# Seven products for eight: the in-projection of a state-space mixer in a part of its own

## The chip, the cores and the metric

The kernel runs on one core of a Trainium2 chip. The metric is the device time of one execution in microseconds; of a kernel the median of several executions is told. Before the change it was 983.28 us, the median of 3 runs (982.39 to 983.92). A core has five engines that run side by side, each with an in-order queue of its own: TensorE (PE, matmuls), VectorE (DVE), ScalarE (ACT), GpSimd (POOL) and SyncE (SP), which here issues all DMAs. Matmuls write to PSUM, eight banks of 512 fp32 columns on 128 partitions; all else lies in SBUF.

## The reference, cut to what matters

One layer of a bidirectional Mamba-2 mixer, all in float32, 1024 tokens, model width 1024, inner width 2048, 32 heads of 64 in 8 groups, state 128, chunks of 128 tokens:

```
u    = rmsnorm(x, norm_w)                            # (1024, 1024)
proj = u @ w_in                                      # z 2048 | x 2048 | B 1024 | C 1024 | dt 64
x, B, C = silu(conv5(x | B | C) + bias)              # depthwise, centred, over tokens
dt   = softplus(dt_raw + dt_bias);  a = -exp(a_log)
y    = x * D
for direction in (forward, backward):                # chunked scan, per group g and chunk c
    y += (C B^T * decay) @ (x dt)                    # inside a chunk, per head
    y += (C @ state) * exp(cumsum a)                 # from the chunks before
    state = state * chunk_decay + B^T @ (x dt decay)
y    = groupnorm(y * silu(z)) * norm
out  = rmsnorm(x + y @ w_out, final_norm_w)
```

## The kernel before, in words

A float32 product is made from three matmuls in the faster fp32r type: each operand is split into a high part (ACT casts it) and a low part (DVE subtracts), and hi*hi, hi*lo and lo*hi are added up in PSUM. The matmuls of the scan are plain fp32; each of them shows as two in the trace.

Start (`load_x` and the loop at L281): eight tiles of 128 tokens are normalised, transposed on PE (L295) and split into `us`, which holds u with channels on partitions for two halves of 512 tokens. Beside it the z product of group 0 runs, together with dt.

In-projection (`inproj`, a generator that is advanced piece by piece): for a group g the units B, C, x0, x1 (128 channels each: 2 halves x 8 k-tiles x 3 matmuls of 512 columns, L180) and z (`z_unit`, 8 token tiles x 24 matmuls of 256 columns, L157). `conv` takes a unit out of PSUM: ACT makes the middle tap (L190), DVE the four others straight from PSUM (L196, 1022 or 1023 columns), ACT a tanh (L199), DVE the closing product (L200). `load_split` (L122, L123) splits the weights, 1024 columns an operation.

Scan (`ssd_units(g)`): first backwards over the chunks, `token_major(c)` (three PE transposes of x0, x1, B, L404, and an ACT copy, L407), `state` (L390, L393) and `update` (L383, L385) for the backward direction; then forwards. `mix(c)` loads the rows of the decays as `fb`, broadcast over the partitions (two slots, L415), ACT adds (L419), DVE selects (L421), ACT takes the exponential (L424), and DVE multiplies with C B^T (L429). Then PE makes the state part `pyo` (L462) and the inner part `pyd` (L468), DVE and ACT put `y` together (L471, L479, L481), the gate (L486), ACT squares into `pyd` (L488), POOL takes the power -1/2 (L85), ACT scales (L490), DVE transposes blocks of 32 x 32 (L493) and SP writes y to DRAM in runs of 128 bytes (L496). PSUM: `ps_ip` has two slots of two banks, `ps_g` four of one bank for all else.

While group g is scanned, the projection of group g + 1 is pulled in after the steps named in `AT` (L501 to L507), so the two lie beside each other. In the last group's scan four token tiles of the out projection (`out_unit`, first half of k) are pulled in instead; the other 12 follow. The order of instructions on each engine is fixed when the program is made, by a planner that takes the program's order as priority; what stands under `tc.high_priority` goes ahead.

Of the kernel before, what the change touches and what calls it, by code (L numbers as in the profile page):

```python
# [31 lines left out]
def kernel(  # L32
# [25 lines left out]
    ps_g = ctx.enter_context(tc.tile_pool(name="ps_g", bufs=4, space=PSUM))  # L58
# [12 lines left out]
    cfb = const.tile([P, 2, NC, NH], F32, name="cfb")  # L71
    ecs = const.tile([P, 2, NC, NH], F32, name="ecs")
    wdt = const.tile([P, 2, NC, NH], F32, name="wdt")
    dcy = const.tile([P, 2, NC, NH], F32, name="dcy")
    dtb = const.tile([P, NC, NH], F32, name="dtb")

    rows_d = dram.tile([2 * NC * NH, P], F32, name="rows_d")
    y_d = dram.tile([DI, L], F32, name="y_d")

    def rstd_of(pool, ss, n, eps, name):  # L80
# [31 lines left out]

    def load_split(srcs, kk, n, name):
        raw = wp.tile([P, kk, n], F32, tag="raw", name=name + "r", bufs=2)
        at = 0
        for src in srcs:
            m = src.shape[2]
            nc.sync.dma_start(out=raw[:, :, at:at + m], in_=src)
            at += m
        hi = wp.tile([P, kk, n], R32, tag="wh", name=name + "h", bufs=4)  # L120
        lo = wp.tile([P, kk, n], R32, tag="wl", name=name + "l", bufs=4)
        nc.scalar.copy(hi, raw)  # L122
        nc.vector.tensor_tensor(out=lo, in0=raw, in1=hi.bitcast(F32), op=ALU.subtract)  # L123
        return hi, lo

    def load_cm(col, name):
        return load_split([w_in[:, :, col:col + P]], NK, P, name)

    def load_z(g):

        n, ks = (CW + 2 * NH, (0, 3, 6, 8)) if g == 0 else (CW, (0, 4, 8))
        at = []
        for i, (k0, k1) in enumerate(zip(ks, ks[1:])):
            srcs = [w_in[:, k0:k1, g * CW:(g + 1) * CW]]
            if g == 0:
# [7 lines left out]
    cms = {}  # L143

    def z_unit(g, c0, wz):

        w, n = (512, 2) if g == 0 else (CW, 4)
        pz = ps_ip.tile([P, n, w], F32, tag="ip", name=f"pz{g}_{c0}")
        m = CW + 2 * NH if g == 0 else CW
        for i in range(n):  # L150
            tok = slice((c0 + i) % 4 * P, ((c0 + i) % 4 + 1) * P)
            uh, ul = us[(c0 + i) // 4]
            at = 0
            for k in range(NK):
                hi, lo = wz[k]
                for a, b in ((uh, hi), (uh, lo), (ul, hi)):
                    nc.tensor.matmul(pz[:, i, 0:m], a[:, k, tok], b,  # L157
                                     start=at == 0, stop=at == 3 * NK - 1)
                    at += 1
        gt = gates[g, c0 // 4]  # L160
        pzg = pz[:, :, 0:CW]
        gt = gt[:, c0 % 4:c0 % 4 + n]
# [3 lines left out]
        if g == 0:  # L166
            for i in range(n):
                nc.vector.tensor_tensor(
                    out=v[:, :, c0 + i, :],
                    in0=pz[:, i, CW:CW + 2 * NH].rearrange("p (d h) -> p d h", d=2),  # L170
                    in1=dtbias, op=ALU.add)
        return n

    def cm_matmul(ps, w, half):
        hi, lo = w
        uh, ul = us[half]
        n = 0
        for k in range(NK):
            for a, b in ((hi, uh), (hi, ul), (lo, uh)):
# [470 lines left out]
```

## Time and profile before

| | |
|---|---|
| median of 3 runs | 983.28 us (982.39 to 983.92) |
| profiled execution | 985.42 us |
| its span, first to last instruction | 983.7 us |
| PE busy | 945.5 us, 96% |
| DVE busy | 727.9 us, 74% |
| ACT busy | 539.2 us, 55% |
| POOL busy | 53.8 us, 5% |
| granted clock of PE | 0.999 of full speed |
| moved by DMA | 107.62 MB, 16 engines busy 41.5% |

The busy time of an engine is the time in which at least one of its instructions ran; instructions of one engine overlap a little, matmuls a good deal, so that what one costs in a row of its like is read from the distance of their starts.

### The profile page before, as it was taken

Reading aid. Unit: us, or ns where it says so; the run is one execution under the profiler, and the core shown is the slowest. Engines: PE = TensorE matmul, PEld = TensorE weight load, DVE = VectorE, ACT = ScalarE, POOL = GpSimd, SP = SyncE. Lnnn points to the kernel's source line nnn. Section 1 sums busy time; section 2 is a strip of 40 time slices with the busy share of each in tenths; the row PEclk is TensorE's granted clock in tenths of the full one; section 3 lists DMA queues with packets and bytes.
Section 4 is the critical chain, followed back from the end, with each engine's and each line's share of the span. In section 5 each row is a group of like instructions: output and inputs, shape, how many; then the busy total and the mean of one; then the engine's idle time right before and its main releaser. Section 6 shows DMA issues by size and latency. Waiting matters only on the chain.

```text
span 983.7 us, 15133 instructions
## 1 busy us (share of the span) xinstructions
PE 945.5 (96%) x5220; PEld 806.1 (82%) x5220; DVE 727.9 (74%) x1552; ACT 539.2 (55%) x1458; POOL 53.8 (5%) x88
## 2 busy tenths in 40 slices
PE   5999999999999999999999999999999999999997
PEld 5987778877887798778887988788889878888886
DVE  4688889867986887688868886888688988552322
ACT  5435567636673767366736673676367876431211
POOL 1100000000000000000000100010001001000000
PEclk9999999999999999999999999999999999999999
DMA  7334134422452345134513352336325686684321
GB/s 223 95 86 97 43 70 94 111 70 70 101 120 53 74 99 124 49 75 98 126 52 82 86 129 63 78 80 126 96 64 142 172 264 174 200 278 142 118 85 65
DMA packets 157325, 107.62 MB, mean 109 GB/s; under 512 B 75248, under 2 KB 133312, under 8 KB 157248
## 3 DMA queue, kind: packets, MB, share of 16 engines
q1 hardware_dynamic: 157248, 106.65, 41.5%
q8 instruction: 41, 0.67, 0.3%
q14 instruction: 36, 0.29, 0.1%
HBM read 89.58 MB, written 17.04 MB: 108 GB/s over the span
## 4 chain that ended last, share of the span: by engine, by line
PE 56%; DVE 12%; DMA 12%; ACT 12%; issue 6%; POOL 2%; SPq 1%; DVEq 0%; POOLq 0%; ACTq 0%
PE po L562 16%; PE ipx L180 12%; PE ipC L180 9%; DMA fb<-rows_d 7%; PE ipB L180 7%; ACT yo L479 3%; DVE x L196 3%; ACT fb L424 2%; PE pz L157 2%; PE pyo L462 2%; PE pyd L468 2%; PE sb L393 2%; ACT fb L419 2%; DVE mt L429 1%; PE sf L393 1%
## 5 line engine op out<-in xcount | busy, mean ns | idle before, releaser
L479 ACT ACTIVATE yo<-pyo,ecs 128x64 f32<-128x64 f32 x448 | 103.1, 320 | 35.8 <-PE pyo L462 30.2
L419 ACT ACTIVATE fb<-fb,cfb 128x128 f32<-128x128 f32 x256 | 85.1, 399 | 55.1 <-DMA fb<-rows_d 49.6
L424 ACT ACTIVATE fb<-fb,cfb 128x128 f32<-128x128 f32 x256 | 84.0, 398 | 3.8 <-DVE fb L421 3.7
L196 DVE SCALAR_TENSOR_TENSOR x<-ipx,prm,x 128x1022 f32<-128x1022 f32 (+1 forms) x64 | 81.1, 1268 | 3.7 <-ACT x L190 3.6
L157 PE MATMUL pz<-wz_1l,uh 128*128 128x256 f32 (+1 forms) x248 | 73.0, 294 | 2.0 <-DVE wz_1l L123 2.0
L157 PE MATMUL pz<-wz_0h,ul 128*128 128x256 f32 (+1 forms) x248 | 73.3, 296 | 0.4 <-DVE ul L301 0.2
L157 PE MATMUL pz<-wz_0l,uh 128*128 128x256 f32 (+1 forms) x248 | 72.0, 290 | 0.0
L157 PE MATMUL pz<-wz_0h,uh 128*128 128x256 f32 (+1 forms) x248 | 71.2, 287 | 0.0
L157 PE MATMUL pz<-wz_1h,ul 128*128 128x256 f32 (+1 forms) x248 | 70.9, 286 | 0.0
L468 PEld LDWEIGHTS pyd<-xb,mt 128*128 128x128 f32 x512 | 66.7, 191 | 4.9 <-DVE mt L429 1.8
L157 PE MATMUL pz<-wz_1h,uh 128*128 128x256 f32 (+1 forms) x248 | 70.4, 284 | 0.0
L471 DVE SCALAR_TENSOR_TENSOR y<-xb,coef,pyd 128x64 f32<-128x64 f32 x256 | 62.5, 273 | 10.5 <-PE pyd L468 10.3
L468 PE MATMUL pyd<-xb,mt 128*128 128x64 f32 x512 | 64.7, 269 | 0.0
L429 DVE TENSOR_TENSOR mt<-fb,pcb 128x512 f32<-128x512 f32 x64 | 43.1, 681 | 15.3 <-PE pcb L427 13.0
L385 DVE TENSOR_TENSOR pb<-pb,sb 128x256 f32<-128x256 f32 x48 | 19.8, 412 | 42.0 <-PE sb L393 41.1
L421 DVE COPY_PREDICATED fb<-trif,fb 128x512 f32<-128x512 uint32 x64 | 47.1, 736 | 3.7 <-ACT fb L419 3.6
L157 PEld LDWEIGHTS pz<-wz_1l,uh 128*128 128x128 f32 x248 | 46.9, 189 | 3.4 <-DVE wz_1l L123 3.2
L157 PEld LDWEIGHTS pz<-wz_0h,ul 128*128 128x128 f32 x248 | 47.2, 190 | 1.3 <-DVE ul L301 1.1
L571 DVE TENSOR_TENSOR h<-po,h 128x1024 f32<-128x1024 f32 (+2 forms) x10 | 10.1, 1011 | 51.3 <-PE po L562 51.3
L157 PEld LDWEIGHTS pz<-wz_0h,uh 128*128 128x128 f32 x248 | 47.1, 190 | 0.5
L157 PEld LDWEIGHTS pz<-wz_0l,uh 128*128 128x128 f32 x248 | 47.1, 190 | 0.0
L157 PEld LDWEIGHTS pz<-wz_1h,ul 128*128 128x128 f32 x248 | 46.9, 189 | 0.2
(511 smaller groups left out, 2667.5 us busy)
## 6 DMA issues: line engine op xcount, KB each, us to landing
fb<-rows_d SPq DMA_DIRECT2D x128, 256.0 KB, 4.3
y_d<-yt SPq DMA_DIRECT2D x256, 32.0 KB, 2.0
wo<-in_ssd_w_out_dram SPq DMA_DIRECT2D x16, 512.0 KB, 4.2
yt<-y_d SPq DMA_DIRECT2D x16, 512.0 KB, 5.1
xt<-in_x_dram SPq DMA_DIRECT2D x8, 512.0 KB, 5.9
h<-in_x_dram SPq DMA_DIRECT2D x8, 512.0 KB, 4.8
h_d<-h SPq DMA_DIRECT2D x8, 512.0 KB, 3.0
h<-h_d SPq DMA_DIRECT2D x8, 512.0 KB, 3.6
```

The costliest lines, as they stand in the source:

```text
L157: nc.tensor.matmul(pz[:, i, 0:m], a[:, k, tok], b, start=at == 0, stop=at == 3 * NK - 1)
L180: nc.tensor.matmul(ps[:, half * 512:(half + 1) * 512], a[:, k, :], b[:, k, :], start=n == 0, stop=n == 3 * NK - 1)
L196: nc.vector.scalar_tensor_tensor(out=acc[:, o], in0=ps[:, i], scalar=w(k), in1=acc[:, o], op0=ALU.mult, op1=ALU.add)
L393: nc.tensor.matmul(ps[:, 0:CW], xb[:, CW:CW + P], xw, start=True, stop=True)
L419: nc.scalar.activation(out=ef[:, h], in_=ef[:, h], func=AF.Identity, bias=cfb[:, 1, c, hsl(g, h)])
L421: nc.vector.copy_predicated(ef, trif.bitcast(U32).unsqueeze(1).broadcast_to([P, HG, P]), fb[:, 0])
L424: nc.scalar.activation(out=ef[:, h], in_=ef[:, h], func=AF.Exp, bias=cfb[:, 0, c, hsl(g, h)])
L429: nc.vector.tensor_tensor(out=mt, in0=ef, in1=pcb[:, 0:P].unsqueeze(1).broadcast_to([P, HG, P]), op=ALU.mult)
L468: nc.tensor.matmul(pyd[:, cs], mt[:, h, :], xb[:, cs], start=True, stop=True)
L471: nc.vector.scalar_tensor_tensor(out=y[:, cs], in0=xb[:, cs], scalar=coef[:, h:h + 1], in1=pyd[:, cs], op0=ALU.mult, op1=ALU.add)
L479: nc.scalar.activation(out=yo[:, cs], in_=pyo[:, d * CW + h * HD:d * CW + (h + 1) * HD], func=AF.Copy, scale=ecs[:, d, c, hsl(g, h)])
L562: nc.tensor.matmul(pos[i], l_, r_[:, cols[i]], start=k == 0 and a == 0, stop=k == NO - 1 and a == 2)
```

## The change

x, B and C of all groups are made first, in 16 pairs (B with C, x0 with x1), and kept in DRAM; the scan loads them afterwards. A pair of 128-column units times two halves of 512 tokens, with the 1024 channels in two halves of four k-tiles, is a 2 x 2 block product; it is made by seven block products of four k-tiles (Winograd's form of Strassen's scheme) where there were eight. t1 to t4 are the sums on the side of u, made once: t1 to t3 on POOL from the normalised tiles in the start (s1, s2, s3, each transposed on PE and split), t4 on POOL after the start. The sums on the side of the weights (s1 to s4) are made on POOL for each pair, and POOL makes three of the seven low parts. Partial results go from one PSUM bank to another by ACT copies and DVE sums, and later matmuls add to them.

`keep_tm` transposes x and B by blocks of 32 x 32 on DVE and writes them token by token with four DMAs in runs of 128 bytes; C and B go to DRAM as they are. The scan loads `xb` of each chunk, B and C, so the PE transposes and ACT copies of `token_major` go. The decays follow the first pair's products. The z products of groups 1 to 7 are pulled into the scan, one token tile at a time, at eight steps a group. The gates of group 0 and a quarter of u pass through DRAM between the parts. PSUM: `ps_g` two slots (mix and pyd), `ps_x` one of two banks for the first part (with `ps_ip` a ring of three), in its place `ps_h` two slots for state and pyo in the second. The start takes the tiles in the order 0, 4, 1, 5, ... . w_out is loaded two k-tiles to a tile. Cut to its core:

```diff
-    ps_g = ctx.enter_context(tc.tile_pool(name="ps_g", bufs=4, space=PSUM))
+    ps_g = ctx.enter_context(tc.tile_pool(name="ps_g", bufs=2, space=PSUM))
...
+    xb_d = dram.tile([NG, L, 3 * P], F32, name="xb_d")
+    bc_d = dram.tile([NG, 2, P, L], F32, name="bc_d")
...
+    wp = ctx.enter_context(tc.tile_pool(name="wp", bufs=9))
+    c4 = ctx.enter_context(tc.tile_pool(name="c4", bufs=5))
...
+            s1 = small(f"s1_{c0}")
+            nc.gpsimd.tensor_tensor(out=s1, in0=ub[:, lo_], in1=ua[:, lo_], op=ALU.subtract)
...
+            for n, (s, dst) in enumerate(((s1, t1), (s2, t2), (s3, t3))):
+                to_cm(s, dst, tok, f"pt{c0}_{n}")
...
+        put("a11", a11, False)
+        s1 = combine("s1", a21, a22, ALU.add)
+        put("s1", s1, False)
+        s2 = combine("s2", s1, a11, ALU.subtract)
+        put("s2", s2, False)
+        put("a12", a12, False)
+        s3 = combine("s3", a11, a21, ALU.subtract)
+        put("s3", s3, True)
+        s4 = combine("s4", a12, s2, ALU.subtract)
+        put("s4", s4, True)
+        put("a22", a22, True)
...
+    def product(ps, w, u_, fresh):
+        hi, lo = w
+        uh, ul = u_
+        n = 0
+        for k in range(4):
+            for a, b in ((hi, uh), (hi, ul), (lo, uh)):
+                nc.tensor.matmul(ps, a[:, k, :], b[:, k, :], start=fresh and n == 0, stop=n == 11,
+                                 skip_group_check=True)
+                n += 1
...
+    def pair_products(w, name):
+        c1 = ptile(name + "1", w)
+        c11, c12 = c1[:, 0:512], c1[:, 512:1024]
+        pw = pst(name + "w")
+        product(c12, w["a11"], b11, True)
+        with tc.high_priority(offset=HP):
+            nc.scalar.copy(c11, c12)
+        product(pw, w["s1"], t1, True)
+        p5 = tw.tile([P, 512], F32, tag="p5", name=name + "p5")
+        with tc.high_priority(offset=HP):
+            nc.scalar.copy(p5, pw)
+        product(c12, w["s2"], t2, False)
+        product(c11, w["a12"], b21, False)
+        c2 = ptile(name + "2", w)
+        c21, c22 = c2[:, 0:512], c2[:, 512:1024]
+        with tc.high_priority(offset=HP):
+            nc.vector.tensor_tensor(out=c12, in0=c12, in1=p5, op=ALU.add)
+            nc.scalar.copy(c22, c12)
+        product(c22, w["s3"], t3, False)
+        product(c12, w["s4"], b22, False)
+        with tc.high_priority(offset=HP):
+            nc.vector.tensor_tensor(out=c21, in0=c22, in1=p5, op=ALU.subtract)
+        product(c21, w["a22"], t4, False)
+        return c1, c2
...
+        nc.vector.transpose(tt.rearrange("p b j -> p (b j)"), acc)
+        dst = xb_d[g].rearrange("(b i) c -> i b c", i=32)
+        for a in range(4):
+            nc.sync.dma_start(out=dst[:, :, off + 32 * a:off + 32 * a + 32],
+                              in_=tt[32 * a:32 * a + 32])
...
+    for n, (g, nm) in enumerate(pairs):
+        nxt = load_unit1(*pairs[n + 1]) if n + 1 < len(pairs) else None
+        if nxt is None:
+            wb.close()
+        ps = pair_products(w, f"{nm}{g}")
+        if n == 0:
+            rows_v = decays()
+        w = nxt
+        for i, p_ in enumerate(ps):
+            if nm == "x":
+                keep_tm(conv(p_, 2 * g + i, f"x{i}_{g}"), g, i * P, f"x{i}t_{g}")
+            else:
+                acc = conv(p_, 16 + 8 * i + g, f"{nm[i]}_{g}")
+                nc.sync.dma_start(out=bc_d[g, i], in_=acc)
+                if i == 0:
+                    keep_tm(acc, g, CW, f"Bt_{g}")
...
-            pxb = pst(f"pxb{g}_{c}")
-            for i, src in enumerate((x0, x1, bt)):
-                nc.tensor.transpose(out=pxb[:, i * P:(i + 1) * P],
-                                    in_=src[:, c * P:(c + 1) * P], identity=ident)
             xbs[c] = sp.tile([P, 3 * P], F32, tag="xb", name=f"xb{g}_{c}", bufs=9)
-            nc.scalar.copy(xbs[c], pxb[:, 0:3 * P])
+            nc.sync.dma_start(out=xbs[c], in_=xb_d[g, c * P:(c + 1) * P, :])
...
-    AT = (2, 6, 9, 11, 13, 15)
+    AT = (2, 5, 8, 10, 11, 13, 14, 15)
```

## Rows read from the trace of the kernel before

**Rows 1.** The page: busy time of the engines, share of the span.

```profile
PE 945.5 (96%) x5220; PEld 806.1 (82%) x5220; DVE 727.9 (74%) x1552; ACT 539.2 (55%) x1458; POOL 53.8 (5%) x88
```

**Rows 2.** Chain of waits, 431 to 450 us: shares by line.

```profile
by line: PE ipx L180 69.4%; PE pyo L462 10.3%; PE pyd L468 8.8%; PE sf L393 7.1%; PE pcb L427 3.7%; ACT yo L479 1.1%; issue 0.8%
```

**Rows 3.** A stretch: us, busy PE, PEld, DVE, ACT, POOL, granted clock, DMA share, GB/s.

```profile
333.97:624.30 290.33, 280.99 (x1634) 241.71 (x1633) 231.71 (x529) 175.81 (x510) 15.30 (x25) 1.00 0.36 88
```

**Rows 4.** Timeline of POOL: start, us, instruction, [idle before, releaser].

```profile
140.75 0.55 POOL L85 TENSOR_TENSOR y_0r<-y_0m,neghalf 128x1 f32<-128x1 f32 x1 [108.49 <-DVE y_0m L82]
...
449.30 0.55 POOL L85 TENSOR_TENSOR y_2r<-y_2m,neghalf 128x1 f32<-128x1 f32 x1 [10.21 <-DVE y_2m L82]
453.97 1.46 POOL L85 TENSOR_TENSOR y_3r<-y_3m,neghalf 128x1 f32<-128x1 f32 x1 [4.12 <-DVE y_3m L82]
...
719.29 0.55 POOL L85 TENSOR_TENSOR y_0r<-y_0m,neghalf 128x1 f32<-128x1 f32 x1 [39.04 <-DVE y_0m L82]
...
797.68 0.66 POOL L85 TENSOR_TENSOR y_0r<-y_0m,neghalf 128x1 f32<-128x1 f32 x1 [25.58 <-DVE y_0m L82]
```

**Rows 5.** Timeline of PE: the first of B, matmuls of 512 columns, transposes.

```profile
51.21 0.39 PE L180 MATMUL ipB<-uh,wB0l 128*128 128x512 f32 x1
...
308.71 0.40 PE L180 MATMUL ipC<-ul,wC3h 128*128 128x512 f32 x1
...
309.41 0.40 PE L180 MATMUL ipC<-ul,wC3h 128*128 128x512 f32 x1
...
310.07 0.38 PE L404 MATMUL pxb<-ident,x 128*128 128x128 f32 x2
310.29 0.27 PE L404 MATMUL pxb<-ident,B 128*128 128x128 f32 x1
```

**Rows 6.** Timeline of DVE, pieces in which it did not wait.

```profile
430.04 0.68 DVE L429 TENSOR_TENSOR mt<-fb,pcb 128x512 f32<-128x512 f32 x1
430.64 0.42 DVE L486 TENSOR_TENSOR y<-y,gate 128x256 f32<-128x256 f32 x1
...
434.73 0.42 DVE L486 TENSOR_TENSOR y<-y,gate 128x256 f32<-128x256 f32 x1
435.07 0.73 DVE L421 COPY_PREDICATED fb<-trif,fb 128x512 f32<-128x512 uint32 x1
...
453.81 1.22 DVE L123 TENSOR_TENSOR wz_1l<-wz_1r,wz_1h 128x1024 fp32r<-128x1024 f32 x1
454.94 1.28 DVE L196 SCALAR_TENSOR_TENSOR x<-ipx,prm,x 128x1023 f32<-128x1023 f32 x1
456.13 0.43 DVE L493 STREAM_TRANSPOSE yt<-y 128x256 f32<-128x256 f32 x1
456.50 1.24 DVE L196 SCALAR_TENSOR_TENSOR x<-ipx,prm,x 128x1023 f32<-128x1023 f32 x1
```

**Rows 7.** Groups of instructions: count, busy us, mean ns, idle before.

```profile
L190 ACT ACTIVATE x<-ipx,prm 128x1024 f32<-128x1024 f32 x16 | 19.2, 1202 | 1.5 <-PE ipx L180 1.5
L300 ACT CAST uh<-pu 128x512 fp32r<-128x512 f32 x16 | 8.6, 596 | 1.7 <-PE pu L295 1.7
...
L103 POOL TENSOR_SCALAR_AFFINE_SELECT trif<-ones 128x128 f32<-128x128 f32 x1 | 0.3, 293 | 0.0
```

**Rows 8.** Busy time in a stretch, columns as in rows 3.

```profile
772.00:797.00 25.00, 24.31 (x127) 19.85 (x126) 23.69 (x46) 17.63 (x37) 0.10 (x1) 1.00 0.80 231
```

**Rows 9.** DMAs: issues, KB each, median us from issue to landing.

```profile
fb<-rows_d SPq DMA_DIRECT2D x128, 256.0 KB, 4.3
y_d<-yt SPq DMA_DIRECT2D x256, 32.0 KB, 2.0
```

**Rows 10.** Timeline of ACT.

```profile
436.89 1.27 ACT L424 ACTIVATE fb<-fb,cfb 128x128 f32<-128x128 f32 x4
...
440.92 1.31 ACT L419 ACTIVATE fb<-fb,cfb 128x128 f32<-128x128 f32 x4
```

**Rows 11.** Waits: who waited for whom, us in total, times, longest.

```profile
ACT fb L419 <- DMA fb<-rows_d: 49.6, 26, 4.1
```

More of the change, by code (lines that the diff above doesn't have):

```diff
@@ L142 @@
-    gates = {}
[L143 to L162, printed above, removed]
+    dec = main.enter_context(tc.tile_pool(name="dec", bufs=1, side="right"))
@@ new lines, with split, z_products @@
+    t1 = ublock(up, "v", "t1")
+    t2, t3 = (ublock(tw, n, n) for n in ("t2", "t3"))
+    b12 = ublock(tw, "t4", "b12")
+    def split(src, hi, lo, pool_engine=False):
+        nc.scalar.copy(hi, src)
+        (nc.gpsimd if pool_engine else nc.vector).tensor_tensor(
+            out=lo, in0=src, in1=hi.bitcast(F32), op=ALU.subtract)
+    gates = {}
+    def z_products(pz, c, wz, m):
+        tok = slice(c % 4 * P, (c % 4 + 1) * P)
+        at = 0
+        for k in range(NK):
+            blk = ((b11, b12), (b21, b22))[k // 4][c // 4]
+            uh, ul = (u_[:, k % 4, tok] for u_ in blk)
+            hi, lo = wz[k]
+            for a, b in ((uh, hi), (uh, lo), (ul, hi)):
+                nc.tensor.matmul(pz[:, 0:m], a, b, start=at == 0, stop=at == 3 * NK - 1)
+                at += 1
@@ L165, in z_unit @@
                                        op0=ALU.add, op1=ALU.mult)
[L166 to L179, printed above, removed]
-                nc.tensor.matmul(ps[:, half * 512:(half + 1) * 512], a[:, k, :], b[:, k, :],
-                                 start=n == 0, stop=n == 3 * NK - 1)
-                n += 1
@@ L229, in inproj @@
-    def inproj(order, nxt):
-        for i, u in enumerate(order):
-            w, nxt = nxt, None
-            after = {(0, "z"): 2}.get(u, 1 if u[1] == "z" else 0)
-            work = run_unit(*u, w)
-            for j in range(after):
-                next(work)
-                yield
-            nxt = load_unit(*order[i + 1]) if i + 1 < len(order) else None
-            yield from work
     def every(it, n):
@@ new lines, with psh @@
+    wp2 = ctx.enter_context(tc.tile_pool(name="wp2", bufs=2))
+    bp = main.enter_context(tc.tile_pool(name="bp", bufs=2))
+    first.close()
+    ps_h = ctx.enter_context(tc.tile_pool(name="ps_h", bufs=2, space=PSUM))
+    sp = main.enter_context(tc.tile_pool(name="sp", bufs=2, side="right"))
+    b12 = ublock(up, "v", "b12b")
+    for i, part in enumerate(b12):
+        nc.sync.dma_start(out=part.rearrange("p k t -> p (k t)").bitcast(F32), in_=b12_d[i])
+    def psh(name):
+        return ps_h.tile([P, 512], F32, tag="h", name=name)
@@ L497, in ssd_units @@
             yield
[L499 to L502 removed]
+    for i in range(2):
+        gates[0, i] = big(f"gate0r{i}", (P, 4, CW))
+        nc.sync.dma_start(out=gates[0, i], in_=gate_d[:, 4 * i:4 * i + 4])
+    stream = z_stream()
+    AT = (2, 5, 8, 10, 11, 13, 14, 15)
+    every(stream, 2)
     for g in range(NG - 1):
```

441 lines of the change are left out of this document (252 added, 189 removed).

## The prediction

> **What bounds the kernel now.** I read the busy shares first: PE 945.5 us of the 983.7 us span, DVE 727.9, ACT 539.2 [rows 1]. A busy PE need not be the bound, so next the chain of waits in one stretch of the scan: 69% of it is the in-projection of x on PE, 30% the scan's own matmuls, 1% ACT, and only 0.8% is issue [rows 2]. PE is the bound there, and the next group's projection fills each gap that the scan leaves. Third, the engines over three whole groups: 290.3 us, with PE 281.0, DVE 231.7, ACT 175.8 [rows 3]; for one group 96.8 us, PE 93.7, DVE 77.2, ACT 58.6. Last the milestones: POOL's power instruction of chunk 0 comes once a group, at 140.75 for group 0, 719.29 for group 6, 797.68 for group 7 [rows 4]: six periods of 96.4 us, then 78.4, then 186.0 to the end of the span.
>
> The change takes work from PE, but it also takes the two loads apart: a group's projection no longer runs beside the scan of the group before. So each half is priced by its own slowest engine.
>
> **First part, PE.** Matmuls of 512 columns stand 0.233 us apart (308.71 to 309.41 is three steps) [rows 5]. A group had 4 x 48 of them, 44.8 us. Now it has two pairs of 7 x 12, 2 x 19.6 = 39.2 us. Saved over the run: 192 matmuls, 44.8 us.
>
> **First part, the others.** DVE starts its next operation 1.19 us after a tap (454.94 to 456.13), 1.13 after one on 1024 columns from SBUF (453.81 to 454.94), 0.60 after one on 512 (430.04 to 430.64), 0.34 after one on 256 (434.73 to 435.07) [rows 6]. A pair of x tiles takes 8 taps 9.5, 2 closing products 2.3, 4 of the weight splits 2.4, 2 seeds (c12 plus p5, c22 less p5) 1.2, and 2 block transposes of 1024. The transpose of 256 holds DVE 0.37 (456.13 to 456.50) [rows 6]; four of those are 1.5, a plain 1024 is 1.13; I take 1.2, nearer the plain one. Sum 17.8, and 16.6 for a pair of B and C, 17.2 on average against PE's 19.6. ACT has 10 operations on 512 at 0.60 and 4 on 1024 at no more than 1.2 [rows 7], under 11. POOL gets 4 sums and 3 splits of 512. No row has one so wide: four times the 128-column affine select of 0.29 [rows 7] is 1.17, the upper end, the power instruction's 0.55 [rows 4] the lower; I take 1.17, since the work grows with the columns: 8.2 us a pair, hidden. (By the Trainium skill, GPSIMD Engine Reference, section 3.1, 2048 columns take 4.50 us; a quarter, 1.12, is an estimate.)
>
> So PE sets the first part if the hand-overs inside a pair are covered. The tightest: after the third product DVE adds p5 and ACT copies into c22, 0.60 + 0.60, while PE has one product (2.8 us) to run. If each engine is held by one long operation first (1.19 and 1.2) that is 3.6, a stall of 0.8; all later products stand behind it, as PE is in order. I take 0.7 a pair, between nothing and 0.8, since DVE is nearly full: 20.3 us a pair, 16 pairs 325 us. The ring of three tiles is wide enough: c2 of a pair needs the taps of c1 of the pair before, 4 x 1.19, and has 14 us. The decays run beside the first products as they ran beside the first group's projection.
>
> POOL and DVE can hold each other: the power instruction takes 0.55 us at 449.30, but 1.46 at 453.97, while DVE's split, which reads two SBUF operands, ran from 453.81 for 1.22 [rows 4, 6]. The Trainium skill (SBUF — State Buffer, Who interferes with whom) says that a DVE instruction with two SBUF inputs and a GpSimd instruction that reads SBUF exclude each other for a whole instruction; by that rule, the trace agrees. The price of it is rival C.
>
> **Start.** The first B matmul starts at 51.21 [rows 5]. The start gets 48 more transposes; two take 0.22 us (310.07 to 310.29) [rows 5], so 5.3 us, all put on the path: 56.5. The 12 sums on POOL that feed them (14 us) lie beside the z products, and the 12 for t4 beside the first six products (16.8 us); without that cover each costs up to its 14.
>
> **Scan, a group.** 192 transposes (21 us of PE) and the 64 ACT copies behind them go. What is left on an engine is its share of rows 3 less the projection. DVE: 77.2 less 16 taps (19.0), 4 closing products and 4 weight splits (8 x 1.13): 49.2 us, gates and z splits included. ACT: 58.6 less 12 operations on 1024 columns, up to 1.2 each [rows 7], and the 8 copies: about 45. PE: 93.7 less 44.8 and 24 transposes (2.6): 46.3. DVE is late next; with nothing lost a group takes 49.2. How full can it be? From 772 to 797 it was busy 23.7 of 25.0 us, 95% [rows 8]; over the three groups 80%, but there PE was the bound. I take 94%, nearer the stretch in which it was pressed: 52.5 us. Only buffers order the next group's backward pass behind this forward pass (nine slots for xb, eight for pb, two each for bt and ct), so its 7.4 us of DVE (21 x 0.34 and a little) can fill gaps.
>
> The loads that replace the transposes (64 of xb, 16 of bt and ct) pass through SP's queue with fb and y: an xb load that waits for its slot holds fb and the y writes behind it, and ACT waits for fb. Writes in runs of 128 bytes, as y's, land after 2.0 us [rows 9]; the 96 new ones have four times the runs, 8 us at most, and all but the last group's are read much later. The PSUM rings of two: a chunk's pyd waits for the Square of the chunk before, behind eight short matmuls, seven DVE operations of 256 columns or fewer (at most 0.34 each [rows 6], 2.4 us) and the Square itself; that is below the 5.2 that DVE needs for a chunk ((49.2 - 7.4) / 8).
>
> **Between the parts.** PE's last product leaves DVE about one and a half conversions and two transposes (11 us), then a backward pass of 7.4 and a chunk, 5.2: 24 us to the first power instruction.
>
> **End.** From group 6's chunk 0 to group 7's it was 78.4 with PE full. Now DVE has 49.2 without z (4.7), plus 8 splits of w_out and 2 of y (10 x 1.13): 56, and an out unit on PE among it; I take 64, between that and 78. Then nothing changes: 186.0.
>
> **Sum**, against the profiled execution: 56.5 + 325 + 24 + 6 x 52.5 + 64 + 186 = 970.5 us of span, where it had 983.7. That execution took 985.4 in all, 1.7 more than its span, and stands 2.1 above the median of 983.3; so the median comes to 970 us.
>
> **Rivals.**
> (B) Slower: the two fb buffers bound the scan. A slot's round is 4.3 from issue to landing [rows 9], ACT 1.31, DVE 0.73, ACT 1.27, DVE 0.68 [rows 6, 10]: 8.3 us, 4.1 a chunk with two slots; and each of the five hand-overs can wait behind other work on engines 80 to 94% full. For it: ACT already waits 49.6 us for fb, 26 times, up to 4.1 [rows 11], and the queue gets more loads. Against it: a chunk has passed in 4.7 us (449.30 to 453.97) with taps on DVE as well [rows 4]. At 6.3 us a chunk a group takes 8 x 6.3 + 7.4 = 57.8: 5.3 more six times and 1.7 in the first, 1003 us. It decides from a chunk of 5.9 us (a group of 54.7), where nothing is gained.
> (C) Slower: DVE and POOL exclude each other in the first part. If each of six DVE operations a pair (4 splits, 2 closing products) waits out a POOL operation, 7.0 us, DVE needs 24.2 instead of 17.2 and PE waits: 16 x 3.9, 1032. With one meeting in two it is 20.7, inside the forecast. That POOL has over half of its time free speaks against it.
> (D) Faster: pairs at 19.8, groups at 50 (DVE 98% full): less 8, 15 and 2, 945 us.
>
> **How the numbers follow.** What lies within 0.2% (2 us) a measurement of this kernel can't tell from no change. Chances: forecast 0.48, within 955 to 986; B 0.28; C 0.10; D 0.14. Of the forecast 0.42 is clearly faster, 0.04 within the bound, 0.02 slower; of B 0.25 slower, 0.02 within, 0.01 faster; C is slower, D faster. Faster 0.57, same 0.06, slower 0.37. The range is 942 to 1018: half of D's lower side, B's upper tail and most of C stay out, some 0.17.
>
> **What would show it.** Right: 512-column matmuls 0.233 apart with a short gap or two a pair; power instructions of chunk 0 some 52 us apart; DVE over 90% busy in the scan and PE idle there. B shows as ACT idle before the first operation on fb, released by DMA; C as DVE's splits started late behind POOL, and PE gaps at the seeds. The forecast falls if groups come over 55 us apart or pairs over 21.5.

## The result, and the profile after

The changed kernel takes 1164.9 us (four runs, 1162.7 to 1167.0) against 983.3 (982.4 to 983.9): a ratio of 1.185 with an interval of 1.182 to 1.1875. It is 182 us slower. I had forecast 970 with a range of 942 to 1018, and gave 0.37 to slower. The profiled execution took 1162.7 with a span of 1161.0.

The page of the changed kernel answers [rows 1]: PE's busy time has not gone down but its share has, from 96% to 82%.

```profile
PE 950.8 (82%) x4890; PEld 798.0 (69%) x4890; DVE 835.4 (72%) x1687; ACT 585.2 (50%) x1573; POOL 253.0 (22%) x228
```

The same view's slices (40 of 29 us; busy share in tenths, below it the granted clock) show dips in the first half, where PE was to be full:

```profile
PE   4894689588958966861999998989887779999997
PEclk9797899889979998995999999999995688999999
```

Three of POOL's power instructions of chunk 0, as in [rows 4], the first for group 0, then groups 6 and 7:

```profile
573.56 0.66 POOL L85 TENSOR_TENSOR y_0r<-y_0m,neghalf 128x1 f32<-128x1 f32 x1 [82.58 <-DVE y_0m L82]
...
913.22 0.66 POOL L85 TENSOR_TENSOR y_0r<-y_0m,neghalf 128x1 f32<-128x1 f32 x1 [14.26 <-DVE y_0m L82]
...
989.59 0.55 POOL L85 TENSOR_TENSOR y_0r<-y_0m,neghalf 128x1 f32<-128x1 f32 x1 [29.85 <-DVE y_0m L82]
```

These, the first product (74.96) and the last (514.0) cut the span into the terms of the forecast. The engines in each, columns as in [rows 3]:

```profile
0.00:74.96 74.96, 53.18 (x296) 48.85 (x297) 37.96 (x60) 29.46 (x55) 26.79 (x32) 0.86 0.48 150
74.96:514.00 439.04, 339.81 (x1371) 262.69 (x1369) 328.46 (x304) 165.37 (x236) 176.99 (x124) 0.91 0.35 81
514.00:573.56 59.56, 25.88 (x170) 24.36 (x169) 32.23 (x59) 17.89 (x46) 0.00 (x0) 0.71 0.73 209
573.56:913.22 339.66, 305.47 (x2036) 277.43 (x2035) 293.44 (x928) 260.21 (x911) 33.25 (x49) 0.92 0.64 161
913.22:989.59 76.37, 61.82 (x252) 48.29 (x252) 58.09 (x164) 48.95 (x164) 5.32 (x9) 0.82 0.66 178
989.59:1161.00 171.41, 164.61 (x773) 136.38 (x771) 85.21 (x175) 63.29 (x165) 10.63 (x16) 0.99 0.55 167
```

```
term                     forecast  measured   difference
start                       56.5      75.0      +18.5
16 pairs                   325       439.0     +114.0
between the parts           24        59.6      +35.6
six groups of scan         315       339.7      +24.7
last group's step           64        76.4      +12.4
end                        186       171.4      -14.6
sum                        970.5    1161.0     +190.5
```

The first part makes three fifths of the miss. It was forecast as full of PE, and no engine is full in it: PE 77%, DVE 75%.

### The profile page after: what moved, and what is told of

The parts are those of the page before. It is cut to its first block, busy times and chain, and to the rows that moved or that the text cites. A ratio compares the mean times of both kernels' runs of the same rounds, so it can differ in the third digit from the quotient of the medians.

```text
span 1161.0 us, 15429 instructions
## 1 busy us (share of the span) xinstructions
PE 950.8 (82%) x4890; PEld 798.0 (69%) x4890; DVE 835.4 (72%) x1687; ACT 585.2 (50%) x1573; POOL 253.0 (22%) x228
## 4 chain that ended last, share of the span: by engine, by line
PE 48%; DVE 18%; ACT 11%; DMA 8%; issue 7%; POOL 6%; SPq 1%; DVEq 0%; POOLq 0%; ACTq 0%
PE po L709 14%; PE x L295 9%; PE pz L145 9%; PE BC L295 6%; DMA fb<-rows_d 5%; PE pyd L606 3%; DVE x L350 3%; PE pyo L600 2%; ACT yo L617 2%; DVE B L350 2%; ACT fb L557 2%; PE sb L533 2%; DMA wz<-in_ssd_w_in_dram 2%; DVE C L350 2%; ACT fb L562 1%
## 5 line engine op out<-in xcount | busy, mean ns | idle before, releaser
L562 ACT ACTIVATE fb<-fb,cfb 128x128 f32<-128x128 f32 x256 | 85.1, 394 | 21.6 <-DVE fb L559 21.3
L350 DVE SCALAR_TENSOR_TENSOR x<-x,prm,x 128x1022 f32<-128x1022 f32 (+1 forms) x64 | 81.7, 1276 | 14.9 <-ACT x L344 13.7
L619 DVE TENSOR_TENSOR y<-y,yo 128x256 f32<-128x256 f32 x112 | 46.6, 417 | 3.1 <-ACT yo L617 2.9
L709 PE MATMUL po<-wo0h,yh 128*128 128x512 f32 x128 | 45.9, 434 | 2.5 <-ACT yh L129 2.5
L709 PE MATMUL po<-wo0l,yh 128*128 128x512 f32 x128 | 44.4, 427 | 2.6 <-DVE wo0l L664 2.6
L533 PE MATMUL sf<-xwf,xb 128*128 128x256 f32 x112 | 39.4, 437 | 8.2 <-ACT yo L617 6.0
L709 PE MATMUL po<-wo0h,yl 128*128 128x512 f32 x128 | 44.4, 422 | 1.9 <-DVE yl L130 1.9
L350 DVE SCALAR_TENSOR_TENSOR B<-BC,prm,B 128x1022 f32<-128x1022 f32 (+1 forms) x32 | 40.9, 1279 | 2.8 <-ACT B L344 2.2
L709 PE MATMUL po<-wo1h,yh 128*128 128x512 f32 (+1 forms) x136 | 42.2, 377 | 0.0
L709 PE MATMUL po<-wo1l,yh 128*128 128x512 f32 (+1 forms) x136 | 42.1, 377 | 0.0
L709 PE MATMUL po<-wo1h,yl 128*128 128x512 f32 (+1 forms) x136 | 42.1, 377 | 0.0
```

Source lines behind the costliest of these rows:

```text
L350: nc.vector.scalar_tensor_tensor(out=acc[:, o], in0=ps[:, i], scalar=w(k), in1=acc[:, o], op0=ALU.mult, op1=ALU.add)
L533: nc.tensor.matmul(ps[:, 0:CW], xb[:, CW:CW + P], xw, start=True, stop=True)
L562: nc.scalar.activation(out=ef[:, h], in_=ef[:, h], func=AF.Exp, bias=cfb[:, 0, c, hsl(g, h)])
L709: nc.tensor.matmul(pos[i], l_, r_[:, cols[i]], start=k == 0 and a == 0, stop=k == NO - 1 and a == 2)
```

## The experiments

Each was run once beside the kernel before, which gave 981.4 to 983.5; the four runs of the changed kernel lay within 0.4%, so differences of 5 us or more are read. For the first part I give group lengths: from the last product of one x pair to that of the next, groups 1 to 7, worked out from PE's timelines. Two pairs of seven products are 39.2 us of PE, two of eight 44.8. Group 0, from the first product on, is not in the table: it takes 80.3 us in after and in e1, 55.0 in e2 and 62.5 in e18.

```
after  44.9 55.4 47.6 57.6 47.7 57.8 47.6
e1     45.5 42.0 45.1 51.6 52.2 51.5 42.9   e2  44.8 44.8 44.8 44.8 44.8 51.2 44.8
e5     41.6 40.8 48.8 51.0 50.7 49.1 40.2   e6  45.0 43.2 50.7 50.5 51.9 50.9 41.4
e7     46.2 44.1 48.7 48.5 49.9 51.1 44.3   e9  44.5 50.4 54.2 52.4 53.6 52.4 50.8
e10    43.4 44.9 49.7 50.4 49.2 50.1 50.6   e13 41.8 40.7 46.9 48.3 49.9 51.1 41.4
e14    43.9 40.7 44.8 51.0 51.1 51.1 44.4   e15 48.1 41.2 46.5 53.6 55.1 54.9 44.8
e16    40.4 40.1 50.3 52.0 50.8 48.2 44.3   e17 50.1 45.0 43.9 54.6 50.9 51.4 44.4
e18    39.2 39.2 46.9 53.7 51.8 46.9 37.1
```

### Loads of weights ahead of the stores (e1)

The dips of the changed kernel come once in two groups. One of them, PE then POOL, SP, DVE and ACT of the kernel after:

```profile
322.97 0.40 PE L295 MATMUL BC<-t4h,wBC4a22l 128*128 128x512 f32 x1
...
337.60 0.79 PE L295 MATMUL x<-b11h,wx4a11h 128*128 128x512 f32 x1 [14.23 <-ACT wx4a11h L129]
...
329.53 1.26 POOL L273 TENSOR_TENSOR wx4s<-wx4r 128x512 f32<-128x512 f32 x1 [32.66 <-DVE B L354]
```

```profile
320.93 2.23 SPq L365 DMA_DIRECT2D xb_d<-x1t  x4
323.26 1.25 SPq L261 DMA_DIRECT2D wx4r<-in_ssd_w_in_dram  x2
...
309.59 1.25 DVE L362 STREAM_TRANSPOSE x0t<-x 128x1024 f32<-128x1024 f32 x1
319.66 1.25 DVE L362 STREAM_TRANSPOSE x1t<-x 128x1024 f32<-128x1024 f32 x1
...
335.98 1.06 ACT L353 ACTIVATE C_4t<-C 128x1024 f32<-128x1024 f32 x1 [6.66 <-DVE C L350]
336.94 0.60 ACT L129 CAST wx4a11h<-wx4r 128x512 fp32r<-128x512 f32 x1
```

SP issues x3's stores when DVE's transposes are done (309.59, 319.66 + 1.25), and the load of pair x4's weights stands behind them, at 323.26, when PE is at the last product of the pair before. Then ACT's split of it stands behind a tanh that waits for DVE's taps. PE idles 14.2 us.

```
-            nc.sync.dma_start(out=raw[:, i], in_=w_in[...])
+            with tc.high_priority(offset=2 * HP):
+                nc.sync.dma_start(out=raw[:, i], in_=w_in[...])
```

> The weight loads of the pairs get a higher priority, so that they stand ahead of the stores of x, B and C in SP's queue; nothing else changes. Theory S (a load stands in SP's order behind stores that wait for DVE's conversion two pairs back, and PE waits for the weights): the gaps of 12.8 to 14.4 us ahead of x2, x4 and x6 go, and what follows from them; the first part, 439 us from the first product to the last, falls to 350 to 370, the run to about 1085. Rival D (DVE, 76 us busy of 105 in four pairs, with POOL holding it up, is the bound): the waits move to the seeds, pairs stay above 25 us, the run above 1130.

Measured: 1140.6 us, 24 less than after; the long groups 2, 4 and 6 shrink by 13.4, 6.0 and 6.3, but group 5 grows from 47.7 to 52.2. The queue's order was a cause: the first part falls from 439.0 to 411.1 us, 28 of the 114; the run gains 24, since the stretch between the parts grows from 59.6 to 63.8. The run and the pairs are where rival D put them, though DVE is not full: 147.8 of 200.4 us (241.4 to 441.8). From group 4 on a pair takes 25.9 with the loads early as well: something else is next. The runs e2, e5 to e8 and e12 to e18 keep this edit; e11 is built on e2, and e3, e4, e9 and e10 on the changed kernel.

### Eight plain products in the same two parts (e2)

```
-  (left out: seven products, eight sums, seeds c11, p5, c12, c22, c21; t1 to t4)
+        for c, x1, x2 in ((c1, "a11", "a12"), (c2, "a21", "a22")):
+            for i, (bu, bl) in enumerate(((b11, b21), (b12, b22))):
+                ps = c[:, i * 512:(i + 1) * 512]
+                product(ps, w[x1], bu, True)
+                product(ps, w[x2], bl, False)
```

> The same two parts and the loads first, as in e1, but the pairs are made by the eight plain products: no sums of weights or of u, no t1 to t4, no copies or sums of seeds. Per pair 96 matmuls, 22.4 us, instead of 84. If the scheme itself costs nothing beside its matmuls (theory S): pairs of 22.8, 2 to 3 us longer than in e1, the first product at 52 us instead of 75, the run about 1067 to 1090, within 20 us of e1. If the scheme's sums and seeds are what slows the first part (rival D): pairs of 22.8 against 25 or more in e1, and the run over 50 us faster than e1.

Measured: 1067.2 us, with the kernel before at 981.4. So of 183.5 us the cut into two parts, with its loads and stores, costs 86, the scheme of seven 73 more (e1 less e2), and the order of SP's queue 24. First product at 56.7, last at 431.6, first power at 480.3, six groups 56.2 on average. PE has no gap for whole groups; three of them, columns as in [rows 3]:

```profile
201.22:335.63 134.41, 134.41 (x578) 108.12 (x576) 88.80 (x76) 38.81 (x46) 16.18 (x12) 1.00 0.47 102
```

A group costs 44.8 + 56.2 = 101 in two parts, where the fused kernel took 96.4 [rows 4]: the second part doesn't shrink by what left it.

### The scan's PSUM rings and fb buffers (e3, e4)

```
e3  -            nc.scalar.activation(out=pyd[:, CW:2 * CW], in_=y, func=AF.Square, accum_out=ss)
    +            sq = sp.tile([P, CW], F32, tag="sq", name=f"sq{g}_{c}", bufs=1)
    +            nc.scalar.activation(out=sq, in_=y, func=AF.Square, accum_out=ss)
e4  fb: two buffers -> three
```

> The changed kernel with one edit in the scan: the Square of y writes its values to a buffer in SBUF instead of the second half of pyd, so that pyd's slot (two of them) comes free after DVE's last read. Theory P (the ring of two pyd/pcb slots in PSUM holds the scan): DVE waits 32 us for pyd in all, four a group, so groups fall from 56.6 to about 53.5 and the run by 15 to 25 us. Theory B (the two fb buffers) : no change, 0 to 3 us.

> The changed kernel with three fb buffers instead of two. Theory B of the prediction (fb's round of load, two ACT passes and DVE binds the scan; ACT waits 28 us for fb's loads in all): groups fall from 56.6 to about 53.5, the run by 15 to 25 us. Theory P (PSUM ring of pyd): 0 to 3 us.

Measured: 1177.1 and 1163.9 us. A scan group is 57.0 in e3 and 55.9 in e4, against 56.6. Neither the Square that holds a PSUM tile nor the number of fb buffers sets it. In e4 the last step is 66.3 instead of 76.4, but the end 186.1 instead of 171.4: its sum is no better. e3 is 12 us longer than after, 8 of them in the last step (84.0); why is open.

### The seeds between the products (e5, e7)

```
e5  no copies, no p5: each accumulation starts anew (leaves the seeds out)
e7  c22 <- c12 and c21 <- c22 as ACT copies, p5 added to c12 and c22 by DVE after their last products
```

> On top of e1 (loads first, 26.0 us a pair over pairs 9 to 12, 1140.6 us). Left out: the copies and sums that carry one product over into another (c11, p5, c12 plus p5, c22, c21); each of the four quarters starts from its own product, so the output differs; the 84 matmuls, the sums of weights and all splits stay. Theory H (PE waits in order for seeds that cross ACT and DVE: 1.2 us after the first product and 2.3 to 2.7 before the fifth, in each pair, and the clock falls in the gaps): pairs fall to 20.5 to 21.5, the run to about 1065. Rival W (the weights come late: ring of nine slots, POOL's sums): pairs stay at 24 or more, the run above 1110.

> On top of e1: the same seven products and the same result, with the seeds in another order: ACT copies c12 to c22 before p5 is added and c22 to c21 before the last product, and DVE adds p5 to c12 and c22 at the end, off PE's path. Theory H: the stall before the fifth product (2.3 to 2.7 us) goes to near 0.5, the 1.2 after the first stays; pairs fall to about 24, the run to about 1108. Theory W: pairs within 0.7 us of 26.0.

Measured: 1128.7 and 1142.3 us; e7 is no better than e1's 1140.6, and without any seed the steady groups of e5 (4 to 6) are still 49 to 51. In the stretch of e1 below, PE waits 0.8 to 1.0 us for the first seed of an x pair and 1.9 to 2.5 before the fifth product. Without seeds PE waits elsewhere. The longest waits of PE in e1 and in e5 from 241.4 to 441.8 (engine, line, waited for: us in total, times, longest):

```profile
PE x L296 <- ACT x L332: 9.3, 4, 2.5
PE x L296 <- DVE x L351: 9.1, 3, 3.1
PE BC L296 <- ACT BC L332: 6.3, 3, 2.2
```

```profile
PE x L296 <- DVE x L341: 28.8, 4, 8.7
```

L351 and L341 are the taps, the last operations that read a tile in PSUM; they give back its place in the ring of three. The time won at the seeds is spent at the ring.

### Weights, splits and sums (e6, e13 to e18)

```
e6   ring of split weights 9 -> 13 deep; to make room t3 is t2 (leaves out t3)
e13  a21, a11, a12, a22 stand in for s1 to s4: no sums, four splits a pair (leaves out the sums)
e14  a sum is its first operand: no POOL sums, still seven splits (leaves out the sums)
e15  the sums on DVE          e16  e13 with casts and splits on POOL
e17  all seven casts of a pair on POOL     e18  e13 and e5 together
```

> On top of e1: thirteen slots for the split weights instead of nine; for the room t3 is left out and t2 stands in its place, so the output differs; the start has 16 transposes and 4 sums less. Theory W (ACT's split of a later pair's weight waits for PE to free one of nine slots, and the seed copies and conversions behind it on ACT wait with it): those waits of ACT go, pairs fall from 26.0 to 23 or less, the run to 1090 or less (2 to 4 us of it from the start). Theory H alone: pairs stay within 0.7 us, the run above 1125.

> On top of e1: no sums of weights and four splits a pair instead of seven (s1 to s4 stand for a21, a11, a12 and a22, already split), so the output differs; the seven products with all their seeds, the conversions and the stores stay. Theory W2 (the weights' way over POOL, ACT and DVE, seven splits and four sums through in-order queues, is what PE ends up waiting for): pairs fall from 26.0 to 20.5 to 22, the run from 1140 to 1055 to 1080. Rival H2 (the seeds' hand-overs): pairs stay at 24 or more, the run above 1105.

> On top of e1: POOL's four sums a pair are left out and raw blocks split in their place (seven splits, so the output differs). If POOL's sums (5.1 us a pair and their place in POOL's queue) hold the weights up: pairs fall to 23 or less, the run to 1090 or less. If the seven splits on ACT, DVE and POOL and the nine slots do: pairs stay above 24.5.

> On top of e1: the four sums of weights run on DVE instead of POOL (2.4 us a pair more on DVE, 5.1 less on POOL; same result). If POOL's queue is the cause: pairs at 22 to 24, the run at 1075 to 1110. If DVE's load or its order counts: pairs at 26 or more, the run at 1140 or more.

> e13 (four splits, no sums, seven products with seeds; the output differs) with both halves of each split on POOL: eight operations of some 1.3 us there, 10.2 a pair, and no weight operation on ACT or DVE. Theory L (an operation that waits for PE in ACT's or DVE's queue holds up the conversions behind it, and PE waits for those): in groups 4 to 6 pairs fall from 24.9 in e13 to 21 to 22.5; the seeds still wait for PE on DVE and ACT. Theory K (the chain of a conversion itself: ACT, four taps, tanh, close, transpose, store): 24.5 or more.

> On top of e1 (full scheme, same result): the seven casts of a pair move from ACT to POOL, which has then 14 operations, 14 to 18 us a pair; DVE keeps its four low halves. Theory L: ACT's waits for PE go, pairs in groups 4 to 6 fall from 25.9 to 22 to 24.5, the run from 1140 to 1100 to 1125. Theory K, or POOL's queue in place of ACT's: 25.5 or more, the run at 1135 or more.

> e13 and e5 together: four splits, no sums, no seeds, seven products of 84 matmuls (the output differs). Theory L, with splits and seeds each enough to hold the conversions: pairs in groups 4 to 6 fall to 20 to 22 (25.3 in e5, 24.9 in e13), the run to 1055 to 1080. Theory K: 24 or more, the run above 1100.

Measured: 1136.7, 1117.5, 1119.7, 1147.0, 1128.7, 1153.6 and 1108.4 us. Taking work off helps in the first groups, and in e18 groups 1 and 2 run at PE's 39.2. But from group 4 to 6 each of the seven takes 47 to 55 us a group, with 7 splits or 4, sums or none, on whichever engine. My last theory (L), that an operation which waits for PE and stands in ACT's or DVE's queue ahead of a conversion sets the pair, was to bring e18's steady pairs down to 20 to 22; they stayed at 24.9. That doesn't refute it, for e18 keeps four casts on ACT that wait for PE. An example of it in e18, DVE and ACT, then PE:

```profile
318.86 5.23 DVE L330 SCALAR_TENSOR_TENSOR x<-x,prm,x 128x1022 f32<-128x1022 f32 x4 [1.28 <-ACT x L324]
...
332.43 0.62 ACT L129 CAST wx6a11h<-wx6r 128x512 fp32r<-128x512 f32 x1 [8.71 <-PE BC L285]
...
336.28 1.05 ACT L333 ACTIVATE x_4t<-x 128x1024 f32<-128x1024 f32 x1
...
337.36 1.49 DVE L334 SCALAR_TENSOR_TENSOR x<-x_4t,x 128x1024 f32<-128x1024 f32 x1 [0.73 <-ACT x_4t L333]
```

```profile
347.42 0.77 PE L285 MATMUL x<-b11h,wx5a11h 128*128 128x512 f32 x1 [7.00 <-DVE x L330]
```

The taps of a tile end at 324.1. Its tanh could start, but ACT's next instruction is a cast that waits 8.7 us until PE frees a weight slot, and the tanh comes at 336.3. The tiles behind it are late, and PE then waits 7.0 for the ring. The two stretches of e18, four pairs before the fall and eight in it:

```profile
135.50:213.90 78.40, 78.40 (x338) 63.07 (x337) 63.34 (x54) 27.44 (x32) 10.42 (x8) 1.00 0.47 104
213.90:413.10 199.20, 173.25 (x697) 133.38 (x695) 126.88 (x108) 54.55 (x64) 20.57 (x16) 0.95 0.46 95
```

In the second DVE is busy 64% and ACT 27%: no engine is full, and PE waits for tiles. Conversion goes one tile at a time. ACT's first operation (1.2), the four taps (5.2), tanh (1.1), the closing product (1.2), the transposes (1.25): 9.9. The next tile starts 0 to 3 us after the closing product or the transposes; 8.9 to 10.2 a tile were seen with nothing between, so some 20 a pair against PE's 19.6: no slack at all. Over eight pairs e18 takes 24.9 a pair and e1 25.05, some 12.5 a tile.

What adds the 2.5 a tile can be seen in part. In e18 DVE idles 72.3 us of the second stretch (16 tiles), and during 34 of these ACT or DVE itself stands at an operation that PE must release, nearly all of them casts for a weight slot: 2.1 a tile. In e16, which has no weight operation on the two, it is 41 of 71.8 us (228.9 to 430.1, 16 tiles), 2.6 a tile, and there the seeds hold the conversions. In the lines of e16 below, ACT's copy of a seed waits 7.1 us for PE, the tanh behind it comes late, and with it DVE's closing product; later DVE itself waits 5.4 at a seed. ACT, then DVE:

```profile
334.22 0.57 ACT L312 COPY BC<-BC 128x512 f32<-128x512 f32 x1 [7.12 <-PE BC L287]
334.70 1.06 ACT L345 ACTIVATE C_4t<-C 128x1024 f32<-128x1024 f32 x1
```

```profile
335.80 1.23 DVE L346 SCALAR_TENSOR_TENSOR C<-C_4t,C 128x1024 f32<-128x1024 f32 x1 [5.50 <-ACT C_4t L345]
...
349.39 0.70 DVE L327 TENSOR_TENSOR BC<-BC,BC5p 128x512 f32<-128x512 f32 x1 [5.38 <-PE BC L287]
```

Each of the runs left one kind of such operations in the queues: casts in e18, seeds in e16. **Open:** whether the pair falls to 20 without both; e16 without seeds wasn't run. A deeper ring of the five buffers that the conversions share wasn't tried either.

### Program order for SP (e9, e10)

```
e9   loads of the weights issued two pairs ahead, loads and stores kept in program order on SP
e10  e9 with the seeds of e7
```

> The changed kernel with SP's queue in a fixed order in the first part: the weight load of pair m stands right behind the stores of pair m-3 (in the changed kernel it stands behind those of pair m-2 or m-1 in every second group, in e1 ahead of those of pair m-4, so that there the stores wait for the load's slot and hold the conversion's buffers). Nothing else changes. Theory S (the one queue ties loads and stores together, and either of them late stops PE): pairs fall from 26.2 to 22 to 23, the run to about 1090. Rival H (hand-overs of the seeds and the order on ACT and DVE set the pair whatever SP does): pairs stay at 25 or more, the run above 1125.

> e9 with the seeds of e7 (DVE's sums off PE's path), both edits together. Theory S with seeds as the second cause: another 1 to 2 us a pair, pairs at 20.5 to 21.5, the run 15 to 30 us under e9. If the seeds hold nothing, as in e7: within 8 us of e9.

Measured: 1160.8 and 1144.8 us: 4 (too little to read) and 20 less than after. In e9 the groups become even from the second on, but at 50 to 54. In e10 they take 49 to 51 from the third on, an x pair 22.0 and a B, C pair 27 to 29, and in the last four of these PE waits 4.9 to 5.0 for DVE's split of the pair's first weight.

### Loads of the second part early (e11, on e2)

```
+    with early(0):     # tc.high_priority(offset=120), around group 0's loads of
+        ...            # b12, wz, bt and ct, xb, the gates, the first two fb
```

> e2 (eight products) with the second part's first loads (b12, gate, z weights, B, C and x of group 0) ahead of the last pair's stores in SP's queue. Theory S for the seam: last product to first power instruction, 49 us in e2, falls to 25 to 30, the run from 1067 to about 1045. If DVE's last conversions and the backward pass set it: 45 or more, no change.

Measured: 1078.6 us against e2's 1067.2: worse. The stretch from the last product to the first power is 62 us, not 49. SP and DVE of e11:

```profile
439.50 0.34 SPq L595 DMA_DIRECT2D gate0r<-gate_d  x1
...
438.12 1.25 DVE L318 STREAM_TRANSPOSE x1t<-x 128x1024 f32<-128x1024 f32 x1
```

The gate's load goes to a buffer of the conversions, so it can't be issued before the last transpose, whatever its place in the program. It now stands ahead of the last stores of x, which come at 449.9 and 455.3 where they came at 432.4 and 442.0 in e2, and the scan's loads of x follow them. So the run doesn't tell what the seam would cost with its loads in time.

### The scan's own work (e8, e12, on e1)

```
e8   two of the three products of z left out: 15 us of PE a group
e12  y <- y + yo left out, 14 operations of DVE a group
```

> On top of e1: the gate products of groups 1 to 7 keep one of their three terms (high by high), so the output is less exact: 128 of 192 matmuls of a group's z go, 15 us of PE at 0.119 each; ACT's and DVE's part of z stays. Theory Z (PE's blocks of 24 z matmuls, 2.9 us each, hold up the scan's short matmuls, and PE sets the group of 56.9 us in e1): groups fall to 52 or less, the run by 35 or more. Rival: DVE's order and hand-overs set it: groups stay within 1.5 us, the run falls by less than 10.

> On top of e1: the sums y plus yo in the scan are left out (14 DVE operations of 256 columns a group, 4.8 us; the output lacks the states' part). Theory D2 (DVE, 87% busy, sets a group of 56.9 us through its order): groups fall by about 5, to 52, the run by 35. Rival L (the chain of hand-overs between the engines sets it, and no engine's load): groups fall by less than 2, the run by less than 15.

Measured: 1156.1 and 1126.8 us against 1140.6. In e12 a group is 53.8 against 57.0. I had put the addition at 4.8 us (14 at 0.34); DVE's busy time fell by 4.2 a group, and 3.2 of it came back. In e8 it is 60.0: slower with less work. Four scan groups of e1, then of e8:

```profile
603.51:831.30 227.79, 211.41 (x1447) 195.29 (x1446) 194.88 (x616) 174.53 (x610) 21.74 (x32) 0.94 0.65 159
```

```profile
607.11:847.07 239.96, 185.93 (x803) 146.26 (x802) 195.41 (x620) 173.22 (x610) 21.15 (x33) 0.69 0.61 150
```

DVE's work is the same; what differs beside the products left out is the granted clock, 0.94 and 0.69. So e8 doesn't tell what PE's share in the scan's length is.

## Why the prediction was wrong, step by step

**"So PE sets the first part if the hand-overs inside a pair are covered."** This step failed: 439.0 us instead of 325. Of the 114 us, 40 lie in group 0 (80.3 instead of 40.6, told below), 28 in SP's queue (e1), and 47 stay in groups 1 to 7 of e1. For these I compared sums: DVE 17.2, PE 19.6. DVE's sum was near: 147.8 us of DVE over 200.4 in e1, eight pairs at 25.05, is 18.5. But a tile's conversion is a chain through ACT and DVE, 9.9 us of operations, and tiles pass it one after another. It was the row of [rows 6] in which DVE "did not wait" that I multiplied; it shows what a tap holds, not how long a tile takes. The ring of three, which I called wide enough from the taps alone, is where PE waits once the seeds are gone (e5, e18). What the runs put in the step's place is a chain without slack that operations waiting for PE hold up (e16, e18); that these are all of it is not shown.

**SP's queue in the first part had no term.** I priced stores behind loads in the scan, and not the loads of weights behind the stores of x in the first part. It cost 28 us there and 24 of the run (e1).

**"I take 0.7 a pair"** for the seeds: PE's waits for them in e1 sum to 15.6 us in eight pairs for the fifth product alone, 2.0 a pair. Undersized, but not the cause: e5 is 12 us better than e1, not more.

**"Without that cover each costs up to its 14."** The cover failed, +18.5 and 16 of the 40 us in group 0. In SP's queue the loads of x wait 9.8 us for buffers that POOL's sums give back, and two of them stand behind stores of the gates; PE works 53.2 us before its first product instead of the 40.5 of before, at a clock of 0.86 instead of 1.00. Then the 12 sums for t4; ACT, DVE and PE after:

```profile
96.17 0.62 ACT L129 CAST t4h<-d 128x512 fp32r<-128x512 f32 x1 [6.84 <-POOL d L447]
...
105.16 0.58 ACT L331 COPY BC<-BC 128x512 f32<-128x512 f32 x1
...
94.66 0.67 DVE L330 TENSOR_TENSOR BC<-BC,BC0p 128x512 f32<-128x512 f32 x1
...
105.79 0.79 PE L295 MATMUL BC<-t3h,wBC0s3h 128*128 128x512 f32 x1 [16.27 <-ACT BC L331]
```

DVE's part of the seed is done at 95.3; ACT's copy of it comes at 105.2, behind casts of t4 that wait for POOL. I had looked at when t4 is needed, not at what stands behind its casts in ACT's queue. e2 starts at 56.7, the 56.5 forecast, but by luck: it has neither the sums nor the 48 transposes that I had put at 5.3, so the new start is 5.5 longer than before's 51.21 without them as well, and no run says why.

**"The decays run beside the first products"** failed too. They stand on PE in the second pair, and PE waits for DVE's part of them:

```profile
131.71 1.19 PE L409 MATMUL pa<-dt,trif 128*128 128x256 f32 x2 [8.00 <-DVE dt L406]
```

The 16.3 us above and these 8.0 are 24 of the 40; the rest is not taken apart.

**"Between the parts 24."** This was 59.6. SP, ACT, PE after:

```profile
530.82 2.24 SPq L365 DMA_DIRECT2D xb_d<-x1t  x4
533.15 0.57 SPq L475 DMA_DIRECT2D b12bh<-b_d  x1
...
535.60 1.21 SPq L484 DMA_DIRECT2D wz<-in_ssd_w_in_dram  x2
```

```profile
545.91 0.62 ACT L129 CAST wz_0h<-wz 128x512 fp32r<-128x512 f32 x1 [17.66 <-DMA wz<-in_ssd_w_in_dram]
...
546.58 0.58 PE L145 MATMUL pz<-wz_0h,b11h 128*128 128x256 f32 x1 [32.44 <-ACT wz_0h L129]
...
555.33 0.81 PE L533 MATMUL sb<-xwb,xb 128*128 128x256 f32 x3
```

DVE's tail is 16.8 (514.0 to 530.8) where I had 11. Then the loads, 15.1 to ACT's cast at 545.9, then z in front of the backward pass, 9.4 to 555.3, and 18.2 to the first power where I had 12.6. The loads and z had no term: before, they lay in the projection of the group before.

**"I take 94%"** for DVE in the scan. The work was right: 293.4 over six groups is 48.9 a group, forecast 49.2. The fill was 86%. And I hadn't looked at what the row of the 95% holds: [rows 8] lies in the last group, where PE had the out projection (L562) and DVE the splits of w_out and of y, with no tap among them. A group of the view of that stretch, before:

```profile
L521 DVE SCALAR_TENSOR_TENSOR wo0l<-wo,prm,wo0h 128x1024 fp32r<-128x1024 f32 x6 | 7.7, 1281 | 1.3 <-ACT wo0h L520 1.2
```

With the three splits of y that is 11.4 of DVE's 23.7 us, work that fills gaps and that the groups of the new scan have little of. That its lack makes the difference of 95 and 86% is my reading; no run shows it. The chain of waits of the six groups goes over many lines, and none has a fifth of it:

```profile
by line: PE pz L145 19.3%; DMA fb<-rows_d 12.4%; PE pyd L606 8.1%; issue 5.7%; ACT fb L557 5.3%; PE pyo L600 4.9%; ACT yo L617 4.9%; PE sb L533 4.2%; ACT fb L562 3.2%; DVE y L619 2.3%; PE sf L533 2.3%; DVE fb L559 2.1%; DMA xb<-xb_d 1.8%; A
```

[Rows 2], where one engine had 99%, was a stretch of 19 us and too short to go by: over a whole group of before (431 to 528 us) the chain goes over many lines as well, with 34% on the projection's three.

```profile
by line: PE ipx L180 14.6%; PE ipC L180 11.6%; PE ipB L180 7.9%; issue 7.7%; ACT yo L479 4.4%; DMA fb<-rows_d 4.4%; DMA wx05r<-in_ssd_w_in_dram 4.1%; ACT fb L424 3.8%; DVE C L196 3.7%; DVE x L196 3.7%; PE sb L393 2.5%; ACT fb L419 2.5%; PE 
```

PE was busy 50.9 a group, not 46.3, at a clock of 0.92. Which of these sets the 56.6 is settled only in part: DVE's load for three quarters of what is taken from it (e12), fb's buffers for 0.7 (e4), the Square not (e3).

**Last step and end.** 76.4 + 171.4 = 247.8 against 250: the sum held by luck, its parts did not.

**The rivals.** B had the size (57.8 a group; 56.6 came) and the wrong cause. C's exclusion is there but small: in the first part DVE's split of 512 columns takes 0.68 alone and up to 1.80 beside POOL, and POOL's own operation is 1.26, up to 2.13 beside DVE. By the rule that I drew from the Trainium skill (SBUF — State Buffer, Who interferes with whom), the trace agrees. Over the first part the splits lose some 20 us by it, 1.3 a pair, where C took 7. And e14, without POOL's sums but with its three splits a pair, has the same steady groups. No rival named a chain of conversions or the load of the seam, and the start and the first part alone could have been as forecast: the other terms would still give 1028.6.

## What to carry to other kernels

Price moved work as a chain, with its hand-overs and the number that can be under way, before comparing sums of engines; a sum says who could be the bound, not that the bound is reached. When a fused stage is cut in two, the half that keeps the gaps need not shrink by what has left it (here 101 us a group in two parts, 96.4 before), and loads that lay under the other work come out at the seam: here 86 us without any new arithmetic (e2). For each added instruction list what stands behind it in its queue; here stores ahead of loads on SP, and casts ahead of a seed or a tanh on ACT.

## What the runs showed of the hardware

After a short gap PE's clock can fall. In e1, 3.13 us of idle time precede pair x4; the first five of PE's matmuls come 0.23 to 0.31 us apart, those from the sixth to the twelfth 0.43, where 0.233 is usual [rows 5]: the lower of the two levels, 1.2 GHz. In the product after that it is 0.233 again.

```profile
314.39 0.47 PE L296 MATMUL x<-b11h,wx4a11h 128*128 128x512 f32 x1 [3.13 <-DVE x L351]
...
315.75 0.63 PE L296 MATMUL x<-b11h,wx4a11l 128*128 128x512 f32 x1
316.18 0.63 PE L296 MATMUL x<-b11h,wx4a11h 128*128 128x512 f32 x1
```

The granted clock over these 3.5 us (314.39 to 317.90) is 0.65. From 241.4 to 441.8 this came after seven of e1's fourteen gaps of over 0.5 us and cost 1.5 to 2.5 us each beside the gap. In all PE was busy for 172.3 us there, where 672 matmuls 0.233 apart are 156.8: of the 43.6 us that the eight pairs lose, 28 are gaps and 15.5 matmuls that come slower. The larger case is e8: with a third of z's products the scan's clock was 0.69 and the groups were 3 us longer than with all of them.

A POOL operation on 512 columns takes 1.26 us (the 329.53 row of after), where I took 1.17. The estimate from the Trainium skill (GPSIMD Engine Reference, section 3.1) was 1.12; the measured time decides.
